# Two-layer hybrid backbone: where the second layer's modulation is multiplied

## The chip, the cores and the metric

One core of a Trainium2 chip runs the whole program. The metric is the time of one execution on the device, in microseconds (us); the time of a kernel is the median of its runs. TensorE is called PE, VectorE DVE, ScalarE ACT, GpSimd POOL, SyncE SP; PEld is PE's loading of weights.

## The reference

Two layers work on 256 context and 256 latent tokens of width 1024. Each layer has two sub-layers, a token mixer and a mixture of experts, and both read a modulated norm:

```python
mod_x = jnp.split((sc @ ada_w[l] + ada_b[l])[:, None, :], ADA_CHUNKS, axis=-1)
...
hx = modulate(xx, norm1_g[l], mod_x[0], mod_x[1])
mc, mx = token_mixer(hc, hx, p, lower[l], row, col, lam_init, last)
xx = xx + mod_x[2] * mx
hx = modulate(xx, norm2_g[l], mod_x[3], mod_x[4])
xx = xx + mod_x[5] * expert_choice_moe(hx, moe_router[l], moe_w1[l], moe_w3[l], moe_w2[l])
```

`sc` is silu of the condition (one vector for the latents, one for the context), `ada_w[l]` is 1024 x 6144: six chunks of 1024 columns, numbered 0 to 5. Chunks 0 and 1 are needed before the mixer, 2 at its end, 3 and 4 before the experts, 5 after them. The mixer has four branches, which all read the same modulated tokens through one wide projection: a gated linear attention (GLA) scan, a Hyena convolution, an HGRN2 scan, and a differential attention (two softmaxes, the second subtracted). Each branch's output is multiplied by its matrix, gated by a sigmoid of its own 1024 projected columns, and the four are summed (the merges) and projected out. The experts are 16, each of which takes its best tokens.

## The kernel before, in words

All weights are streamed in f32. Matmuls of the mixer are done as three products of split halves: a weight tile of 128x1024 (512 KB, SP's queue, `load`, L797 to L807) is split into a high part on ACT (L804) and a low part on DVE (L805), and then a column block is 24 matmuls of 128x128 by 128x256 (`col_block`, PSUM tag "d", two buffers). PSUM tags have fixed numbers of buffers: `BUFS = {"d": 2, "s": 3, "m": 2, "a": 1}`. In the trace a tile in PSUM is named by its tag: pd, ps, pm, pa.

A modulation chunk is eight tiles of 128x1024 of ada_w (512 KB each). `Ada.step` (L463 to L474) loads one tile by SP (L466) and multiplies it by the 32 condition columns, four matmuls side by side into 32 partitions each of one "a" tile; the trace records 8 matmuls for a tile. After eight tiles `mod_write` (L444 to L453) copies the result (DVE, L446), transposes it on PE (L425) and adds the bias (DVE, L453). In the second layer chunks 2 to 5 (32 tiles) are done by `AdaBack` (L477 to L495): it has two buffers of 1024 columns, and every call `run(n)` at some place of the mixer lets it do n tiles more. The constants at L31 to L35 set the places: two tiles in the turn and half a tile for each of the eight modulated blocks (`TR`), two with each mixer weight (`ADA`, L806), half with each step of the scans (`SCN`). In the trace all 32 tiles are done before the attention starts, so later calls do nothing.

The turn is the stretch from the last scatter of layer 0's experts to the first column blocks of layer 1 (gk, gq): sums of squares, norms (`rs_tokens`, `bcast_rs`, L760 to L763), modulation of the eight blocks (L764 ff.). Then come the weights in the order gk, gq, gv0, gv1, hq0 and so on: the GLA scan, the HGRN scan, the projections of the attention, the rotations, the attention.

The attention (L1187 to L1223) has eight iterations: four heads by two blocks of 128 queries. An iteration makes two scores on PE (tag "s", L1207), a maximum of each (DVE, L1209), its negative (L1210), an exponential of each with its sum (ACT, L1211), the reciprocals and the weighting (DVE, L1214 to L1216), transposes of the result (PE, tag "m", L1218), their copy (ACT, L1220), and the product with the values, accumulated over four iterations in one more "s" tile. After four iterations the output is normalised (L1230 to L1235, a chain of some twenty small DVE and ACT operations) and transposed (L1246, L1247).

The merges (`merge`, L853 to L872) of branches 0 and 2 follow in the source (L1266, L1267), those of 3 and 1 behind the Hyena branch. A merge has eight steps: column block, tanh (ACT, L858), product of six matmuls with the branch's matrix, and a gated sum (DVE, L866, L870). Which instruction comes when on an engine is decided by a scheduler over the whole program, which interleaves merge blocks with the attention; tiles and buffers are handed out in the order of the source. The product's PSUM tag is chosen at L863: "s" while modulation is left to do, else "a"; since none is left by then, it is "a".

## Time and profile before

| | us |
|---|---|
| median of 3 runs | 2025.32 |
| the runs | 2013.99, 2025.32, 2026.59 |
| the profiled execution | 2021.9 |
| its span in the trace | 2020.1 |
| PE busy in the span | 1859.6 (92%) |
| DVE busy | 801.5 (40%) |
| ACT busy | 526.1 (26%) |

How to read it: a table of stretches gives, for each stretch of the span, the time that each engine was busy (PE, PEld, DVE, ACT, POOL in this order) and in brackets the number of its instructions, then the granted clock of PE (1.00 is full), the share of the DMA engines and GB/s. A timeline row gives start, duration, engine, line, operation, the written tile and what it was read from, and in square brackets how long the engine stood idle before and what ended that. Line L428 is the helper that records every matmul, so matmuls are told apart by their tiles.

### The profile page before, as it was taken

Reading aid. Unit: us, or ns where it says so; the run is one execution under the profiler, and the core shown is the slowest. Engines: PE = TensorE matmul, PEld = TensorE weight load, DVE = VectorE, ACT = ScalarE, POOL = GpSimd, SP = SyncE. Lnnn points to the kernel's source line nnn. Section 1 sums busy time; section 2 is a strip of 40 time slices with the busy share of each in tenths; the row PEclk is TensorE's granted clock in tenths of the full one; section 3 lists DMA queues with packets and bytes.
Section 4 is the critical chain, followed back from the end, with each engine's and each line's share of the span. In section 5 each row is a group of like instructions: output and inputs, shape, how many; then the busy total and the mean of one; then the engine's idle time right before and its main releaser. Section 6 shows DMA issues by size and latency. Waiting matters only on the chain.

```text
span 2020.1 us, 28474 instructions
## 1 busy us (share of the span) xinstructions
PE 1859.6 (92%) x11722; PEld 1089.5 (54%) x11722; DVE 801.5 (40%) x1768; ACT 526.1 (26%) x929; POOL 28.7 (1%) x52
## 2 busy tenths in 40 slices
PE   7999999999999899999897889999998999987877
PEld 3666677887887434434232356788997333221213
DVE  5464638837543313212020345769865111110101
ACT  4432336622232211101000243447443100000000
POOL 0000000000000000000000010001000000000000
PEclk9998999999999899999999999999998999999999
DMA  8744531322326999999999856334568999999999
GB/s 310 224 151 135 177 102 58 105 84 84 122 98 260 359 401 350 380 409 409 409 409 409 314 188 199 105 102 139 198 251 326 409 409 409 409 409 409 409 409 332
DMA packets 154005, 549.03 MB, mean 272 GB/s; under 512 B 11026, under 2 KB 22674, under 8 KB 153108
## 3 DMA queue, kind: packets, MB, share of 16 engines
q1 hardware_dynamic: 153300, 544.08, 71.2%
q0 software_dynamic: 576, 3.15, 0.5%
q8 instruction: 92, 1.51, 0.3%
q14 instruction: 37, 0.30, 0.0%
HBM read 544.03 MB, written 3.15 MB: 271 GB/s over the span
## 4 chain that ended last, share of the span: by engine, by line
PE 71%; DMA 20%; DVE 5%; issue 2%; ACT 2%; SPq 0%; DVEq 0%; ACTq 0%
PE pd L428 41%; PE ps L428 15%; DMA r<-moe_w 9%; DMA base<-moe_w 7%; PE pm L428 6%; PE pa L428 6%; DMA base<-ada_w 2%; PE pm L425 2%; DMA base<-wg 1%; ACT r L804 1%; PE ps L1597 1%; DVE r L805 1%; DMA base<-xT 0%; DVE r L1195 0%; DVE base L1594 0%
## 5 line engine op out<-in xcount | busy, mean ns | idle before, releaser
L428 PE MATMUL pd<-r 128*128 128x256 f32 (+3 forms) x2976 | 572.3, 363 | 12.0 <-DMA r<-moe_w 7.6
L428 PEld LDWEIGHTS pd<-r 128*128 128x128 f32 (+2 forms) x2976 | 424.7, 184 | 132.0 <-issue 59.3
L428 PE MATMUL pd<-r,r 128*128 128x512 f32 (+3 forms) x1304 | 284.1, 435 | 12.0 <-DMA r<-moe_w 9.4
L805 DVE TENSOR_TENSOR r<-base,r 128x1024 fp32r<-128x1024 f32 x136 | 166.0, 1222 | 160.5 <-ACT r L804 157.4
L428 PEld LDWEIGHTS pd<-r,r 128*128 128x128 f32 (+2 forms) x1304 | 162.7, 167 | 107.6 <-issue 59.3
L804 ACT ACTIVATE r<-base 128x1024 fp32r<-128x1024 f32 x136 | 143.5, 1059 | 268.9 <-PE pd L428 216.2
L428 PE MATMUL ps<-base 32*64 32x64 f32 (+12 forms) x2372 | 178.3, 280 | 12.3 <-DMA base<-hy 4.4
L428 PE MATMUL pd<-r,base 128*32 128x512 f32 (+1 forms) x680 | 166.7, 598 | 12.0 <-DMA r<-moe_w 10.4
L428 PEld LDWEIGHTS ps<-base 32*64 32x64 f32 (+7 forms) x2372 | 113.2, 144 | 73.3 <-issue 43.3
L428 PE MATMUL pm<-base 128*128 128x128 f32 (+12 forms) x660 | 104.7, 326 | 18.3 <-DVE base L1528 5.8
L428 PE MATMUL ps<-r,base 128*64 128x512 f32 (+4 forms) x468 | 98.6, 525 | 13.7 <-DVE base L1598 6.3
L428 PE MATMUL pd<-base 128*32 128x512 f32 (+1 forms) x408 | 100.5, 595 | 6.4 <-DMA base<-moe_w 5.6
L428 PEld LDWEIGHTS pm<-base 128*128 128x128 f32 (+5 forms) x660 | 72.2, 179 | 61.2 <-issue 31.5
L428 PEld LDWEIGHTS pd<-r,base 128*32 128x32 f32 (+1 forms) x680 | 42.0, 122 | 112.1 <-issue 73.9
L1594 DVE TENSOR_TENSOR r<-base,pd 64x512 f32<-64x512 f32 x16 | 10.9, 680 | 214.4 <-PE pd L428 202.2
L1593 ACT ACTIVATE base<-pd 128x512 f32<-128x512 f32 (+1 forms) x32 | 19.0, 594 | 253.7 <-PE pd L428 253.7
L1594 DVE TENSOR_TENSOR base<-base,pd 128x512 f32<-128x512 f32 x16 | 11.0, 688 | 184.6 <-PE pd L428 150.4
L428 PE MATMUL pa<-r,r 128*128 128x512 f32 (+1 forms) x384 | 82.6, 342 | 1.1 <-DVE base L866 1.1
L1644 ACT ACTIVATE base<-ps 32x512 f32<-32x512 f32 (+2 forms) x28 | 14.7, 526 | 252.5 <-PE ps L428 248.0
L1644 ACT ACTIVATE r<-ps 32x512 f32<-32x512 f32 (+2 forms) x32 | 15.4, 480 | 249.9 <-PE ps L428 243.8
L428 PE MATMUL pd<-base,r 128*32 128x512 f32 (+1 forms) x296 | 71.3, 597 | 9.4 <-DMA base<-moe_w 9.4
L428 PE MATMUL pa<-base 128*32 128x256 f32 (+1 forms) x704 | 70.1, 407 | 9.4 <-DMA base<-ada_w 9.2
(241 smaller groups left out, 1633.6 us busy)
## 6 DMA issues: line engine op xcount, KB each, us to landing
r<-moe_w SPq DMA_DIRECT2D x251, 1024.0 KB, 18.2
base<-moe_w SPq DMA_DIRECT2D x131, 1024.0 KB, 17.9
base<-wg SPq DMA_DIRECT2D x152, 512.0 KB, 3.3
base<-ada_w SPq DMA_DIRECT2D x84, 512.0 KB, 4.6
r<-ada_w SPq DMA_DIRECT2D x12, 512.0 KB, 10.3
base<-xT SPq DMA_DIRECT2D x4, 1024.0 KB, 6.2
filters<-r SPq DMA_DIRECT2D x8, 256.0 KB, 4.3
base<-filters POOLq DMA_DIRECT2D x2, 1024.0 KB, 6.4
```

What stands on the lines that cost most here:

```text
L425: T.transpose(out, in_, ident)
L428: return T.matmul(out, lhsT, rhs, start=start, stop=stop, **kw)
L804: A.activation(w[0](), raw(), AF.Copy)
L805: V.tensor_tensor(w[1](), raw(), F(w[0]()), op=OP.subtract)
L1593: A.activation(s_(np_=rows), pa[0:rows, :], AF.Silu)
L1594: V.tensor_tensor(h_(np_=rows), s_(np_=rows), pb[0:rows, :], op=OP.mult)
L1597: T.transpose(p[:, q * rows:q * rows + rows], h_(q * 128, n=128, np_=rows), cs("ident", n=rows, np_=rows))
L1644: A.activation(dst, src, AF.Copy)
```

## The change

`AdaBack` is no longer used; the new `AdaBurst` takes its place. At the end of layer 0's experts it takes as many buffers of 1024 columns as memory gives, up to 16 (there are six), and loads the first tiles. In the turn, `turn` multiplies chunks 2 and 3 in one go (sixteen tiles) and frees the buffers. `run`, still called in `load` and the scans, does nothing. Ahead of the first merge it takes buffers again (there are fourteen) and loads eight tiles; `block`, called before each column block of the merges of branches 0 and 2, multiplies a whole chunk if eight tiles are under way or landed, and issues two more loads. Chunks 4 and 5 are done there. The products of these two merges take the PSUM tag "s".

```diff
--- before.py
+++ after.py
@@ -494,6 +494,63 @@
                 if not self.left:
                     self.buf.free()
 
+    class AdaBurst:
+
+
+        def __init__(self, chunks, per):
+            self.tiles, self.per = [(l, c, k) for l, c in chunks for k in range(KB)], per
+            self.left, self.issued, self.done, self.bufs = len(self.tiles), 0, 0, []
+
+        def run(self, n=None):
+            pass
+
+        def open(self, bufs):
+            self.bufs = bufs
+            self.load(KB)
+
+        def load(self, n):
+            while n and self.issued < len(self.tiles) and self.issued - self.done < len(self.bufs):
+                l, c, k = self.tiles[self.issued]
+                b = self.bufs[self.issued % len(self.bufs)]
+                S.dma_start(out=b(), in_=ins["ada_w"][l][128 * k:128 * k + 128, c * 1024:(c + 1) * 1024])
+                self.issued += 1
+                n -= 1
+
+        def chunk(self, more=0):
+
+            p = ps("a")
+            for k in range(KB):
+                l, c, _ = self.tiles[self.done]
+                b = self.bufs[self.done % len(self.bufs)]
+                for j in range(4):
+                    mm(p[32 * j:32 * j + 32, 0:256], cs_b(k * 32, n=32), b(j * 256, n=256), k == 0, k == KB - 1)
+                self.done += 1
+                self.left -= 1
+                if self.issued < more:
+                    self.load(1)
+            mod_write(l, c, p)
+
+        def block(self):
+
+            if self.issued - self.done >= KB:
+                self.chunk()
+            self.load(self.per)
+
+        def turn(self):
+
+            for _ in range(2):
+                self.chunk(2 * KB)
+            for b in self.bufs:
+                b.free()
+            self.bufs = []
+
+        def close(self):
+            while self.left:
+                self.block()
+            for b in self.bufs:
+                b.free()
+            self.bufs = []
+
 
     def rsqrt_small(x, n, y, t):
 
@@ -760,11 +817,9 @@
             b = rs_tokens(sums.tokens(mem), 2, mem)
             rs = bcast_rs(b, 2)
             b.free()
-            ada_bg.run(TR[1])
+            ada_bg.turn()
         for k in range(KB):
             t = tmp[k % 2]
-            if l:
-                ada_bg.run(TR[2])
             for s in range(2):
                 c = slice(s * 256, s * 256 + 256)
                 sc_, sh = Ac(k * 2 + s, n=1), mod[l](k * 2 + s, n=1)
@@ -850,15 +905,17 @@
             b = ob[br]
             split(src, b(2 * fb * W, n=W), b((2 * fb + 1) * W, n=W))
 
-        def merge(br, first):
+        def merge(br, first, burst=None):
             o = ob[br]
             for d in range(KB):
+                if burst:
+                    burst.block()
                 p = col_block(f"m{br}{d}", t0)
                 g = view(accb, d * W, W) if first and l else mem.take(W, keep_x if first else None)
                 A.activation(g(), p, AF.Tanh, scale=0.5)
                 if d % 4 == 0:
                     load_wb(br, d // 4)
-                p = ps("s" if ada_bg.left else "a")
+                p = ps("s" if ada_bg.left or burst else "a")
                 for fb in range(2):
                     w = [b(((d % 4) * 2 + fb) * 128, n=128) for b in wbs]
                     mm3(p[:, 0:W], w, (o(2 * fb * W, n=W), o((2 * fb + 1) * W, n=W)),
@@ -1261,11 +1318,25 @@
                 ahead.append(b)
 
         run_ahead(AHEAD[l][0])
-        if FL[l]:
+        burst = None
+        if l == 0:
             ada_bg.run()
-        merge(0, True)
-        merge(2, False)
-        ada_bg.run()
+        else:
+            burst = ada_bg
+            tmp, bufs = [mem.take(W) for _ in range(2)], []
+            while len(bufs) < 2 * KB:
+                try:
+                    bufs.append(mem.take(1024))
+                except MemoryError:
+                    break
+            for b in tmp:
+                b.free()
+            burst.open(bufs)
+        merge(0, True, burst)
+        merge(2, False, burst)
+        if burst:
+            burst.close()
 
 
         df, H = mem.take(1024), mem.take(2048)
@@ -1656,14 +1727,11 @@
                                            op0=OP.mult, op1=OP.add)
                 if not last and gr == 3:
                     if d == 0:
-                        b, keep = [b for b in slots if b.mem is mem][:2]
+                        b = [b for b in slots if b.mem is mem][0]
                         slots.remove(b)
                         spare.append(b)
-                        slots.remove(keep)
                         nxt.append(TokenSums(0, [view(b, 512 * i, 512) for i in range(4)], tag="s"))
-                        nxt.append(AdaBack([(1, c) for c in range(2, 6)], keep))
                     nxt[0].step(d)
-                    nxt[1].run(TR[0])
                 if last and gr == 3:
                     S.dma_start(out=outT[:, d * 256:d * 256 + 256], in_=xk(d, 1))
 
@@ -1690,7 +1758,20 @@
                     gather(gr + 1)
             if gr < 3:
                 scatter(gr)
-        for b in spare + slots + mid + [xg[1]] + gone + Pg + ys:
+        for b in slots + gone:
+            b.free()
+        mem.merge()
+        if not last:
+            nxt.append(AdaBurst([(1, c) for c in range(2, 6)], 2))
+            bufs = []
+            while len(bufs) < 2 * KB:
+                try:
+                    bufs.append(mem.take(1024))
+                except MemoryError:
+                    break
+            nxt[1].open(bufs)
+        for b in spare + mid + [xg[1]] + Pg + ys:
             b.free()
         mem.merge()
         dump(f"xmoe{l}", xb[0]())
```

How the change moves instructions is shown at three places. First PE from the end of the gk block on, in the kernel before (pd_6955 is gk, pd_6995 gq, pd_7062 and pd_7112 are the blocks behind, gv0 and gv1; pa_6985 is the second chunk, eight tiles):

```order
L428 MATMUL pd_6955<-r_6809 128x512 x4
L428 MATMUL pa_6985<-base 32x256 x8
L428 MATMUL pd_6995<-r_6809 128x256 x24
L428 MATMUL pm_7022<-base 128x512
L428 MATMUL pm_7026<-base 128x512
L428 MATMUL pa_6985<-base 32x256 x8
L428 MATMUL pd_7062<-r_6809 128x256 x38
L428 MATMUL pa_6985<-base 32x256 x4
L428 MATMUL pd_7062<-r_6809 128x256 x9
L428 MATMUL pa_6985<-base 32x256 x4
L428 MATMUL pd_7062<-r_6809 128x256
L428 MATMUL pd_7112<-r_6809 128x256 x48
```

There each four or eight matmuls of the chunk stand between column blocks. In the changed kernel the end of the turn reads (pd_7002 gk, pd_7031 gq, pd_7078 and pd_7128 the blocks behind, pa_6890 the second chunk):

```order
L428 MATMUL pd_7002<-r_6815 128x512 x3
L428 MATMUL pd_7031<-r_6815 128x256 x2
L428 MATMUL pa_6890<-base 32x256 x4
L428 MATMUL pd_7031<-r_6815 128x256 x9
L428 MATMUL pa_6890<-base 32x256 x4
L428 MATMUL pd_7031<-r_6815 128x256 x5
L425 MATMUL pm_6926<-base 128x128 x2
L428 MATMUL pd_7031<-r_6815 128x256 x8
L428 MATMUL pm_7058<-base 128x512
L428 MATMUL pm_7062<-base 128x512
L428 MATMUL ps_7183<-base 64x64 x3
L428 MATMUL pd_7078<-r_6815 128x256
L428 MATMUL pd_7128<-r_6815 128x256
```

What moved: the last six of sixteen tiles stand among gk and gq, and behind gq there is no pa tile until the merges.

Second, PE in the attention of the kernel before, around the second pair of scores (ps_8760 to ps_8818 are scores, ps_8724 the accumulated output, pd_9233, pd_9270 and pd_9307 column blocks of merges, pa_9222 and pa_9259 products of a merge):

```order
L428 MATMUL pa_9222<-r_7165,r_6813 128x256 x6
L428 MATMUL ps_8724<-base 128x64 x4
L428 MATMUL ps_8760<-r_7165 128x512
L428 MATMUL ps_8765<-r_7165 128x512
L428 MATMUL pd_9233<-r_6809 128x256 x22
L428 MATMUL pa_9259<-r_7165,r_6813 128x256 x6
L428 MATMUL ps_8795<-r_7165 128x512
L428 MATMUL pd_9270<-r_6809,r_6813 128x256 x2
L428 MATMUL ps_8800<-r_7165 128x512
L428 MATMUL pd_9307<-r_6809 128x256 x4
L428 MATMUL pd_9270<-r_6809,r_6813 128x256 x14
L428 MATMUL ps_8818<-r_7165 128x512
```

The blocks with their products stand between the iterations. In the changed kernel the same stretch reads (ps_8706 to ps_8784 are scores, ps_8630 the accumulated output, pm_ the transposed weights, pa_8916 chunk 4):

```order
L428 MATMUL ps_8706<-r_7181 128x512
L428 MATMUL pa_8916<-base 32x256 x3
L425 MATMUL pm_8679<-base 128x128 x4
L428 MATMUL ps_8724<-r_7181 128x512
L428 MATMUL ps_8729<-r_7181 128x512
L428 MATMUL ps_8630<-base 128x64 x4
L428 MATMUL ps_8779<-r_7181 128x512
L425 MATMUL pm_8714<-base 128x128 x4
L428 MATMUL ps_8784<-r_7181 128x512
L428 MATMUL ps_8630<-base 128x64 x4
L425 MATMUL pm_8737<-base 128x128 x4
L428 MATMUL ps_8630<-base 128x64 x4
```

What moved: no column block stands between the iterations from the second to the eighth, only tiles of chunk 4. Seven blocks stand ahead of the first transposes, the first product of a merge (ps_8989) stands behind the scores of the eighth iteration, and nine blocks stand behind the attention.

Third, SP's queue at the start of the second mixer before (L466 is a tile of ada_w, L803 a mixer weight):

```order
L466 DMA base<-ada_w 128x1024 x2
L803 DMA base<-wg 128x1024
L466 DMA base<-ada_w 128x1024 x2
L803 DMA base<-wg 128x1024
L466 DMA base<-ada_w 128x1024 x4
L803 DMA base<-wg 128x1024
L466 DMA base<-ada_w 128x1024 x2
```

and in the changed kernel, up to the first merge's weights (L515 is a tile of ada_w, L858 a mixer weight, L867 a branch's matrix):

```order
L515 DMA base<-ada_w 128x1024 x16
L858 DMA base<-wg 128x1024 x19
L867 DMA base<-wg 128x1024
L858 DMA base<-wg 128x1024 x6
L867 DMA base<-wg 128x1024
L858 DMA base<-wg 128x1024 x2
L515 DMA base<-ada_w 128x1024 x3
L858 DMA base<-wg 128x1024
L515 DMA base<-ada_w 128x1024 x3
L867 DMA base<-wg 128x1024
```

What moved: sixteen tiles are issued in one piece ahead of the mixer weights from gv0 on; the other sixteen stand among the weights of the first merges, behind which later weights queue.

## Rows read from the trace of the kernel before

**Rows 1.** Table of stretches: start:end, length, busy us (instructions) per engine.

```profile
1157.20:1190.50 33.30, 29.56 (x180) 13.26 (x180) 19.26 (x51) 10.64 (x22) 6.44 (x6) 0.90 0.64 209
1190.50:1209.10 18.60, 16.22 (x134) 12.82 (x132) 4.95 (x6) 10.53 (x13) 0.00 (x0) 1.00 0.56 193
1209.10:1235.00 25.90, 25.18 (x382) 14.91 (x382) 19.56 (x56) 10.38 (x24) 1.46 (x5) 1.00 0.61 201
...
1265.70:1283.20 17.50, 17.35 (x244) 13.03 (x243) 14.92 (x42) 9.24 (x20) 0.89 (x3) 1.00 0.36 122
```

**Rows 2.** The same stretches, PE's instructions on the pa tiles alone.

```profile
1157.20:1190.50 33.30, 8.45 (x80) 0.90 0.64 209
1190.50:1209.10 18.60, 2.56 (x32) 1.00 0.56 193
1209.10:1235.00 25.90, 7.55 (x72) 1.00 0.61 201
...
1246.00:1265.70 19.70, 2.35 (x32) 1.00 0.48 160
1265.70:1283.20 17.50, 2.56 (x32) 1.00 0.36 122
```

**Rows 3.** Timeline of PE in the turn, two tiles in a run.

```profile
1186.49 1.07 PE L428 MATMUL pa<-base 128*32 128x256 f32 x16
```

**Rows 4.** Waits of PE from 1190 to 1300 us: total, times, longest.

```profile
PE pa L428 <- DMA base<-ada_w: 3.8, 4, 2.2
```

**Rows 5.** DMA issues of the span: count, size, median us to landing.

```profile
base<-wg SPq DMA_DIRECT2D x152, 512.0 KB, 3.3
base<-ada_w SPq DMA_DIRECT2D x84, 512.0 KB, 4.6
```

**Rows 6.** Timeline of PE in the turn: the transposes of the norms.

```profile
1164.10 1.11 PE L425 MATMUL pm<-base 128*128 128x128 f32 x4 [2.23 <-DVE base L504]
```

**Rows 7.** Timeline of PE, end of the second merge: two blocks.

```profile
1431.68 3.04 PE L428 MATMUL pd<-r,r 128*128 128x256 f32 x24
1434.56 3.02 PE L428 MATMUL pd<-r 128*128 128x256 f32 x24
```

**Rows 8.** Table of stretches: attention and merges, columns as in rows 1.

```profile
1366.60:1434.60 68.00, 65.03 (x513) 62.24 (x514) 59.85 (x152) 44.53 (x85) 5.00 (x9) 1.00 0.45 156
```

**Rows 9.** Timeline of PE in the attention: scores, transposes, scores, scores, output.

```profile
1366.63 0.47 PE L428 MATMUL ps<-r 96*128 96x512 f32 x1 [0.18 <-DVE r L1195]
...
1378.96 0.63 PE L425 MATMUL pm<-base 128*128 128x128 f32 x4 [0.32 <-DVE base L1216]
...
1403.82 0.71 PE L428 MATMUL ps<-r 96*128 96x512 f32 x2
...
1409.85 0.40 PE L428 MATMUL ps<-r 96*128 96x512 f32 x1
...
1418.59 1.10 PE L428 MATMUL ps<-base 128*128 128x64 f32 x8
```

**Rows 10.** Timeline of DVE in the attention: maximum, its negative, weighting.

```profile
1407.68 0.67 DVE L1209 TENSOR_REDUCE base<-ps 128x1 f32<-128x512 f32 x1
...
1408.40 0.14 DVE L1210 TENSOR_SCALAR base<-base 128x1 f32<-128x1 f32 x1
...
1409.06 0.74 DVE L1216 SCALAR_TENSOR_TENSOR base<-base 128x512 f32<-128x512 f32 x1
```

**Rows 11.** Timeline of ACT in the attention: copy of the transposes, exponential.

```profile
1402.27 0.58 ACT L1220 ACTIVATE base<-pm 128x512 f32<-128x512 f32 x1
...
1405.86 0.69 ACT L1211 ACTIVATE base<-ps,base 128x512 f32<-128x512 f32 x1 [1.79 <-DVE base L1210]
```

**Rows 12.** Timelines of DVE and PE: last normalisation's start, transposes behind it.

```profile
1419.74 0.42 DVE L1230 TENSOR_TENSOR base<-ps,base 128x256 f32<-128x256 f32 x1 [1.15 <-PE ps L428]
...
1426.80 0.41 PE L425 MATMUL pm<-base 128*128 128x128 f32 x2
```

**Rows 13.** Table of stretches between mixer and experts, columns as in rows 1.

```profile
1540.00:1560.00 20.00, 11.27 (x93) 9.39 (x91) 11.56 (x44) 4.98 (x10) 0.00 (x0) 0.87 0.77 298
```

More of the change, by code (lines that the diff above doesn't have):

```diff
@@ L1263, in mixer @@
         run_ahead(AHEAD[l][0])
-        if FL[l]:
+        burst = None
+        if l == 0:
             ada_bg.run()
-        merge(0, True)
-        merge(2, False)
-        ada_bg.run()
+        else:
[8 more added lines that the diff above has]
+                b.free()
+            print("merge1", len(bufs))
+            burst.open(bufs)
[3 more added lines that the diff above has]
+            burst.close()
         df, H = mem.take(1024), mem.take(2048)
@@ L1692, in moe @@
                 scatter(gr)
-        for b in spare + slots + mid + [xg[1]] + gone + Pg + ys:
+        for b in slots + gone:
[9 more added lines that the diff above has]
+                    break
+            print("turn", len(bufs))
+            nxt[1].open(bufs)
+        for b in spare + mid + [xg[1]] + Pg + ys:
             b.free()
```

## The prediction

> **What bounds the kernel now.** I read the table of stretches first. TensorE (PE) is busy in nearly all of every stretch of the second mixer: 25.18 of 25.9 us in the GLA scan, 17.35 of 17.5 in the HGRN scan [rows 1]. So work put on PE there, or a wait put in front of it, moves the end. The experts of layer 1 begin where the mixer ends, so I let a microsecond gained or lost in the mixer count fully at the end (rival 3 is the case in which it doesn't).
>
> The same table for the modulation's tiles alone (PSUM name pa) shows where they stand: 80 of 256 records, that is 10 of 32 tiles at 8 records each, up to the end of the gq block, then 4 tiles, 9 in the GLA scan, 4 in the blocks between the scans, 4 in the HGRN scan [rows 2], and one between. A tile costs from 0.64 us (2.56 us for 4) to 0.84 us (7.55 us for 9) where it stands alone among small matmuls. In a run of 16 records it is 0.53 us [rows 3].
>
> The waits of PE from 1190 to 1300 us come last: 3.8 us for landing tiles, four times [rows 4]. A tile takes 4.6 us from issue to landing, a mixer weight 3.3 us [rows 5]. AdaBack has two buffers of 1024 columns, so only two are ever under way.
>
> **The change, part one: what leaves the scans.** All 32 tiles stay; 22 of them leave the stretch from 1190.5 to 1283.2 us.
> - The waits for landing tiles: 3.8 us gained [rows 4].
> - Eight or nine tiles beside column blocks, where PE has no other limit: 2.56 us in 1190.5 to 1209.1, 2.35 us in 1246 to 1265.7 [rows 2], and one tile between, 0.8 us. Together 5.7 us busy, of which I take 5.0; at the packed price (0.53 us) it is 4.8.
> - Nine tiles in the GLA scan: 7.55 us of PE. But VectorE (DVE) is busy 19.56 of the 25.9 us [rows 1] in the scan's own chain, so the most to be had is 25.9 - 19.6 = 6.3 us and the least nothing; I take 3.5, about the middle, since PE and DVE of a scan wait for each other in turn.
> - Four tiles in the HGRN scan: DVE 14.92 of 17.5, so 0 to 2.6 us; I take 1.2.
>
> In the scans, then, the row gives 3.5 and 1.2 us for taking PE work away, because PE is the fuller engine there (25.18 against 19.56 us). The Trainium skill, page "Perfetto Trace Analysis", section "Optimization Strategy", speaks against that: where a kernel has regimes with different limits, it says, interleaving them can pay. By it the tiles lie rightly beside the scans' vector work, nothing is gained there, and the sum below would be 4.7 us higher; the rows agree only in part, since PE is as full as it can be.
>
> **Part two: the turn.** Sixteen tiles now stand among the sums of squares, the gk and the gq block, ten before. Six more at 0.84 us are 5.1 us. PE has a gap of 2.23 us there before the transposes of the norms [rows 6], and PE is busy 29.56 of 33.3 us [rows 1], so a part of the six is free; between 0 and -5.1 I take -2.5. The six buffers are loaded from the end of the experts on. SyncE's queue issues all sixteen loads in one piece ahead of the weights of gv0; the sixteenth needs the buffer of the tenth tile, which PE's order has in the middle of gk and gq, so gv0's weights are not later than now. If they were, the price is one landing, 3.3 us [rows 5].
>
> Gain so far: 3.8 + 5.0 + 3.5 + 1.2 - 2.5 = 11.0 us; with the ends of each term 3.5 to 18.4 us.
>
> **Part three: the merges and the attention.** This decides. In the kernel before, sixteen merge blocks (24 matmuls each, 2.88 us start to start [rows 7]) and their products stand on PE between the eight iterations of the attention. From the first score to the end of the second merge it is 68.0 us with PE busy 65.03 [rows 8]: the chain of an iteration is hidden. In the changed one three things happen.
> - Sixteen tiles come in, most in runs of 8 to 24 matmuls: 16 x 0.53 = 8.5 us of PE (13.4 at 0.84).
> - The products now take the PSUM tag "s" (three buffers) in place of "a". The attention's scores and its accumulated output take "s" too, so the first product stands behind the scores of the eighth iteration. Tanh, product and sum of a block can't finish, but the blocks themselves run ahead: seven of them are done before the first transposes of the attention.
> - The eighth block's weights queue on SyncE behind tiles that wait for memory that the attention still holds. So from the second iteration to the eighth PE has no block at all to do.
>
> PE's own work in those seven iterations is: scores 0.71, transposes 0.63, output 1.10 [rows 9], 2.44 us each, 17.1 in all; with five tiles (2.7) and four products of six matmuls (0.72 each, a quarter of a block's 2.88: 2.9) 22.7 us. The chain of an iteration, all in line, is 0.71 + 0.67 + 0.67 (two maxima) + 0.14 + 0.69 + 0.69 (two exponentials) + 0.74 + 0.63 + 0.58 (copy) + 1.10 = 6.6 us [rows 9 to 11]. Where the kernel now is fastest, three score pairs come 6.03 us apart from first to third, 3.0 us an iteration [rows 9]. With one of three "s" buffers held by the output, one pair is in flight: scores, maxima, one small operation and both exponentials, 3.6 us, before the next. To that I add 0.8 us for the tiles and products that stand between (5.6 us over seven): 4.4 us, nearer to the 3.0 than to the 6.6. Seven times 4.4 is 31 us, so 8 us of PE lie idle (at 3.0 none, at 6.6, 46 us, 23).
>
> Before the first transposes the chain from the second score (about 5 us: maxima, exponentials, weighting) has two blocks as cover, but DVE is then still at the second half's rotations; in the present trace it took from 1366.63 to 1378.96 [rows 9]. I take 3 us idle (0 to 6). After the last output comes the normalisation: from 1419.74 to the transposes at 1426.80 it is 7.1 us [rows 12], now hidden by two blocks. Then the tiles and weights that waited for the attention's memory have to land (4.6 and 3.3 us [rows 5]). Seven products and some tiles cover a part; I take 4 us idle (0 to 10).
>
> Sum of the stage: 8.5 + 8 + 3 + 4 - 3.0 (the idle time that it has now, 68.0 - 65.03) = +20.5 us. The Hyena stage behind it has fewer blocks left beside its convolutions; I put 2 us on it (0 to 5).
>
> **The sum.** 20.5 + 2 - 11 = +11.5 us. The profiled execution took 2021.9 us (its span is 2020.1): 2033.4. The median of the three runs is 3.4 us above it and they spread over 12.6 us, so I say 2037.
>
> **Rivals.**
> 1. *The attention hides itself (not slower).* If iterations come every 3.0 us, as in [rows 9], PE's 22.7 us of work is the longer and the 8 us idle are gone; with the scans shortened to DVE's time the gain is 16, near its upper end of 18.4. For it: the pace of 3.0 us was reached with DVE and ACT serving blocks as well, which they no longer do. Against it: at that pace two pairs overlapped only because other PE work let the chain run ahead, and the order has none. Time: 8.5 + 7 - 3 + 0 - 16 = -3.5, so 2018 on the profiled run, 2015 to 2022. It decides from a pace under 3.2 us.
> 2. *The attention is serial (clearly slower).* At 6 us an iteration seven take 42 us, 11 us more than I count. With PE busy 22.7 of 42 us the clock may fall as well: the stretch 1540 to 1560, busy 11.27 of 20, shows a mean granted clock of 0.87, part of it then at 1.2 in place of 2.4 GHz [rows 13], where 16.22 of 18.6 us busy still show 1.00 [rows 1]. At 0.87 22.7 us of matmul cost 3.4 more. 2037 + 11 + 3 = 2051. The Trainium skill, page "TensorE: Matmul & The Clock Gate", section "Why this matters for your kernels", warns of idle gaps between bursts of matmuls; the two rows agree. For it: the three "s" buffers. Against: DVE and ACT are nearly free of block work in that time.
> 3. *It changes nothing that counts.* Tiles are moved, PE's sum is the same, and the blocks that no longer cover the attention cover the tiles. The gain of 11 then stands against 8.5 + 2, or a shift of the mixer is taken up by the experts' weight stream: 2025. Against it: the order has no block between the iterations.
>
> **How the numbers follow.** Forecast 0.50, rival 1 0.14, rival 2 0.24, rival 3 0.12. A measurement of this kernel can tell about 1%, 20 us, from no change. Forecast and rival 3 stay within it, save the upper fifth of the forecast (losses over 2045); rival 2 lies mostly above; rival 1 rarely goes 20 us below. So slower by over 1%: 0.8 x 0.24 + 0.2 x 0.50 = 0.29; faster 0.07; within 0.64. The range goes from 2014 (rival 1) to 2056 (rival 2 with the tiles at 0.84 us); the forecast's own is 2026 to 2048.
>
> **What would show it.** In the changed profile: no pa tile from the end of gq to the merges, the GLA scan near 22 us, no wait for ada_w there; the time from first score to last output with PE idle a third of it and waits for DVE and ACT (maxima, exponentials, copies); the blocks of the second merge after it back to back; the stage from the first score to the end of the second merge near 89 us in place of 68. If that stage is under 75 us, part three is wrong; if the scans are as long as now, part one is.

## The result, and the profile after

| | before | changed |
|---|---|---|
| median, us (5 runs each) | 2025.32 | 2054.59 |
| runs, us | 2013.99 to 2028.48 | 2044.12 to 2057.08 |
| ratio, 95% interval | | 1.0146 (1.0105 to 1.0187) |
| profiled execution, us | 2021.9 | 2044.12 |

The changed kernel is slower by 1.5%, 29 us by the medians. Its profiled execution is the fastest of its five, so the two traces lie only 22 us apart.

The table of stretches of the changed kernel (columns as in [rows 1]: length, then busy us with counts of PE, PEld, DVE, ACT, POOL, then granted clock, DMA share, GB/s). The first three stretches run from the sums of squares in the turn to the first score of the attention, from there to the end of the attention's last output, and from there to the end of the second merge; the fourth is a part of the second. The end of the second merge is taken one column block behind its last product, in every trace alike.

```profile
1155.10:1348.80 193.70, 184.54 (x1670) 140.22 (x1670) 123.61 (x307) 87.67 (x172) 17.19 (x27) 0.99 0.33 111
1348.80:1402.60 53.80, 42.60 (x237) 32.11 (x238) 34.37 (x102) 26.29 (x58) 3.17 (x6) 0.75 0.40 125
1402.60:1453.90 51.30, 46.89 (x405) 41.82 (x404) 29.18 (x57) 17.73 (x25) 1.16 (x2) 0.97 0.63 204
1372.80:1396.80 24.00, 19.23 (x76) 13.66 (x76) 13.81 (x45) 10.15 (x25) 0.00 (x0) 0.55 0.09 25
```

The same three stretches of the kernel before, from the same view:

```profile
1160.80:1366.60 205.80, 194.58 (x1798) 141.92 (x1798) 123.83 (x314) 86.49 (x170) 15.56 (x26) 0.98 0.45 150
1366.60:1419.70 53.10, 50.12 (x389) 47.51 (x390) 48.69 (x124) 38.41 (x75) 5.00 (x9) 1.00 0.40 139
1419.70:1434.60 14.90, 14.90 (x125) 14.73 (x125) 11.16 (x28) 6.12 (x10) 0.00 (x0) 1.00 0.62 213
```

Up to the first score the change gains 12.1 us (205.8 to 193.7). The attention (first score to last output) lasts as long as before, 53.8 against 53.1 us, but in it PE carries out 237 matmuls in place of 389, and for 24 us of it its mean granted clock is 0.55. What isn't done there comes behind: 51.3 against 14.9 us. Together the two stretches, which answer to [rows 8], take 37 us more. The rest differs by little: the changed trace enters the turn 5.7 us earlier, a stretch that the change doesn't touch, and needs 2.6 us more from the end of the second merge to the end. Without the 5.7 us the traces differ by 28 us, near the 29 of the medians.

The modulation's tiles alone in the changed kernel, columns as in [rows 2]: none between gq and the attention, 128 records (sixteen tiles) in the attention and behind it.

```profile
1187.20:1345.10 157.90, 0.00 (x0) 0.99 0.26 90
1348.80:1402.60 53.80, 5.74 (x48) 0.75 0.40 125
1402.60:1453.90 51.30, 6.09 (x80) 0.97 0.63 204
```

The longest waits of PE in the changed kernel from the first score to the end of the second merge (total, times, longest; L1268 is the exponential, L1277 the copy of the transposes):

```profile
PE pa L428 <- DMA base<-ada_w: 3.4, 4, 1.8
PE ps L428 <- ACT base L1268: 2.8, 4, 2.1
PE ps L428 <- ACT base L1277: 2.4, 4, 0.7
PE pd L428 <- DVE r L860: 2.1, 1, 2.1
```

The waits for landing tiles have moved, not gone: 3.8 us in the scans before [rows 4], 3.4 us here. The timeline of PE inside the attention of the changed kernel, transposes (pm), outputs (x8) and scores (96x512):

```profile
1375.43 1.97 PE L428 MATMUL ps<-base 128*128 128x64 f32 x8
1377.19 1.06 PE L425 MATMUL pm<-base 128*128 128x128 f32 x4
1379.00 1.97 PE L428 MATMUL ps<-base 128*128 128x64 f32 x8 [0.75 <-ACT base L1277]
1380.76 1.06 PE L425 MATMUL pm<-base 128*128 128x128 f32 x4
1382.57 1.97 PE L428 MATMUL ps<-base 128*128 128x64 f32 x8 [0.75 <-ACT base L1277]
1384.30 1.20 PE L428 MATMUL ps<-r 96*128 96x512 f32 x2
1387.56 0.76 PE L428 MATMUL ps<-r 96*128 96x512 f32 x1 [2.06 <-ACT base L1268]
```

An output takes 1.97 us where it took 1.10 [rows 9], four transposes 1.06 where they took 0.63. No column block stands between; PE goes from one small step to the next and waits for the copy or the exponentials.

The pace of the attention is read from the starts of its eight outputs. The first, second, fifth and sixth of the kernel before (the eighth, at 1418.59, is in [rows 9]):

```profile
1380.33 1.10 PE L428 MATMUL ps<-base 128*128 128x64 f32 x8
1389.95 1.10 PE L428 MATMUL ps<-base 128*128 128x64 f32 x8
1402.90 1.10 PE L428 MATMUL ps<-base 128*128 128x64 f32 x8
1411.78 1.10 PE L428 MATMUL ps<-base 128*128 128x64 f32 x8
```

and the first, second, sixth and eighth of the changed kernel (the fifth, at 1382.57, is above):

```profile
1363.16 1.10 PE L428 MATMUL ps<-base 128*128 128x64 f32 x8 [0.73 <-ACT base L1277]
1372.24 1.10 PE L428 MATMUL ps<-base 128*128 128x64 f32 x8 [0.20 <-ACT base L1277]
1393.60 1.97 PE L428 MATMUL ps<-base 128*128 128x64 f32 x8
1401.52 1.10 PE L428 MATMUL ps<-base 128*128 128x64 f32 x8
```

From first to last it is 38.3 us before and 38.4 in the changed kernel. In both, two steps are long, the first to the second output (9.6 and 9.1 us) and the fifth to the sixth (8.9 and 11.0).

### The profile page after: what moved, and what is told of

It reads as the page before. It is cut to its first block, busy times and chain, and to the rows that moved or that the text cites. A ratio compares the mean times of both kernels' runs of the same rounds, so it can differ in the third digit from the quotient of the medians.

```text
span 2042.0 us, 28467 instructions
## 1 busy us (share of the span) xinstructions
PE 1868.6 (92%) x11722; PEld 1096.2 (54%) x11722; DVE 805.2 (39%) x1768; ACT 526.7 (26%) x929; POOL 29.7 (1%) x52
## 4 chain that ended last, share of the span: by engine, by line
PE 71%; DMA 19%; DVE 5%; issue 2%; ACT 2%; SPq 0%; DVEq 0%; ACTq 0%
PE pd L428 41%; PE ps L428 15%; DMA r<-moe_w 9%; DMA base<-moe_w 7%; PE pm L428 6%; PE pa L428 5%; DMA base<-ada_w 2%; PE pm L425 2%; DMA base<-wg 1%; DVE r L860 1%; ACT r L859 1%; PE ps L1668 1%; DMA base<-xT 0%; DVE r L1252 0%; ACT r L1250 0%
## 5 line engine op out<-in xcount | busy, mean ns | idle before, releaser
L428 PE MATMUL pd<-r,r 128*128 128x512 f32 (+3 forms) x1304 | 281.6, 433 | 11.8 <-DMA r<-moe_w 9.4
L1715 ACT ACTIVATE r<-ps 32x512 f32<-32x512 f32 (+2 forms) x32 | 15.4, 480 | 250.1 <-PE ps L428 243.9
L428 PEld LDWEIGHTS ps<-r,base 128*64 128x64 f32 (+2 forms) x468 | 32.8, 140 | 68.9 <-issue 43.5
```

The costliest lines, as they stand in the source:

```text
L428: return T.matmul(out, lhsT, rhs, start=start, stop=stop, **kw)
L1715: A.activation(dst, src, AF.Copy)
```

## The experiments

All are compared with the kernel before on the same chip. Of a kernel's edit the lines that matter are shown; "..." stands for lines left out. "Stage" is the time from the first score to the end of the second merge (67.9 us before, 105.1 us in the changed kernel). Theory T says that the merge products, and with them the blocks, wait for a PSUM buffer that the attention holds; rival R that the sixteen tiles and their loads among the merges cost the time.

| kernel | median, us | ratio to before (95%) |
|---|---|---|
| s_only | 2051.41 | 1.0130 (1.0110 to 1.0150) |
| prod_a | 2064.42 | 1.0176 (1.0148 to 1.0203) |
| prod_a_m | 2028.19 | 1.0019 (1.0001 to 1.0038) |
| turn_only | 2037.54 | 1.0052 (1.0025 to 1.0079) |
| burst_only | 2058.03 | 1.0155 (1.0124 to 1.0187) |
| s_warm | 2065.87 | 1.0189 (1.0160 to 1.0218) |
| late | 2029.54 | 1.0009 (0.9993 to 1.0026) |
| turn_back2 | 2035.65 | 1.0043 (1.0025 to 1.0062) |
| s_nr4 | 2069.86 | 1.0228 (1.0196 to 1.0261) |
| turn6 | 2032.67 | 1.0027 (1.0007 to 1.0046) |
| back6 | 2017.26 | 0.9959 (0.9938 to 0.9979) |
| back4 | 2018.04 | 0.9957 (0.9937 to 0.9977) |

### Which buffer the products take

**s_only**: one condition in the kernel before.

```diff
-                p = ps("s" if ada_bg.left else "a")
+                p = ps("s" if ada_bg.left or (l and br in (0, 2)) else "a")
```

Expected: 

> The kernel before with one word changed: the products of the merges of branches 0 and 2 in layer 1 take PSUM tag s in place of a; the modulation stays in the scans. Theory T (the products wait for the attention's own s tiles, so blocks, tanh and sums back up and nothing covers the attention): 22 to 30 us slower than before, some 2050, first score to end of the second merge near 96 us, and a low granted clock in the attention. Rival R (the sixteen tiles and their loads in the merges cost the time): no change, 2025.

Measured: 2051, and a stage of 97.8 us. Its two stretches, first score to last output and from there to the end of the second merge:

```profile
1365.50:1420.00 54.50, 39.71 (x180) 32.87 (x180) 33.38 (x101) 25.97 (x58) 3.71 (x7) 0.62 0.13 44
1420.00:1463.30 43.30, 40.67 (x327) 39.39 (x328) 28.78 (x52) 18.52 (x26) 0.00 (x0) 1.00 0.53 168
```

No tile of ada_w has moved, yet the picture is that of the changed kernel: 180 matmuls in the attention, a clock of 0.62, the blocks behind it. So the tag alone, without a single tile in the merges, costs 30 us of the 37, and by difference the sixteen tiles and their loads the other 7.

**prod_a**: the changed kernel with the products on "a".

```diff
-                p = ps("s" if ada_bg.left or burst else "a")
+                p = ps("a")
...
```

Expected: 

> The changed kernel with the merge products back on tag a, which the two chunks use too. If tag s alone is the holder: about 2028, since the attention gets its blocks back. Theory T in its wider form (whatever buffer the product needs must not be held by something that ends with the attention; a is held by chunk 4, whose last tiles wait for memory that the attention holds): as the changed kernel, 2050 to 2057. Rival R: 2054.

Measured: 2064, slower even than the wider form of T had it, and no sign of the 2028. The two stretches:

```profile
1354.80:1408.00 53.20, 39.98 (x210) 27.50 (x210) 32.76 (x98) 26.04 (x58) 3.19 (x6) 0.73 0.39 123
1408.00:1474.30 66.30, 57.45 (x430) 50.19 (x431) 31.25 (x61) 17.98 (x26) 1.15 (x2) 0.81 0.51 160
```

Tag "s" isn't special. "a" has one buffer and the program hands it to chunk 4 first; chunk 4 ends only when its last tiles have found memory that the attention gives back (two of their loads stand 12.9 and 16.7 us on SyncE's queue until operations of the attention are done), and every product stands behind it: the first starts at 1417.1, behind the last output at 1408.0.

**prod_a_m**: the chunks of the merges on "m" as well, the products on "a".

```diff
-            p = ps("a")
+            p = ps("m" if not more else "a")
...
-                p = ps("s" if ada_bg.left or burst else "a")
+                p = ps("a")
...
```

Expected: 

> The changed kernel with the merge products on tag a and the two chunks in the merges on tag m, where only short transposes stand. The same tiles, loads and turn. Theory T: the blocks stand between the attention's iterations again, 12 us gained before the first score stay, 8.5 us of tiles come back: 2020 to 2028. Rival R: still over 2045.

Measured: 2028, with the same tiles, loads and turn as the changed kernel. The two stretches (of an execution of 2020, the fastest of its ten):

```profile
1349.40:1399.80 50.40, 46.23 (x351) 42.88 (x351) 45.04 (x119) 35.08 (x71) 4.36 (x8) 1.00 0.54 180
1399.80:1430.60 30.80, 28.37 (x296) 23.63 (x295) 16.79 (x41) 9.27 (x14) 1.16 (x2) 1.00 0.81 282
```

The blocks are back between the iterations, the clock is 1.00, and the stage takes 81.2 us. Against 67.9 the sixteen tiles cost 13 us here: PE is busy 9.6 us more (46.23 + 28.37 against 65.03), and the rest is idle time (50.40 - 46.23 and 30.80 - 28.37, together 6.6, against 3.0 before). 12 us gained and 13 lost leave nothing. The theory of the buffer holds.

### Which part of the change

How far one trace can be trusted here: s_only and s_warm (below) have the same program up to the first score, and from the turn to there their traces take 207.5 and 211.6 us. The changed kernel, prod_a, prod_a_m and late agree better: 193.7, 194.8, 193.8 and 192.6. A difference of 4 us in this stretch, read from one trace each, shows nothing. The stretch in s_only, s_warm and four kernels of this section (turn_only, turn_back2, turn6, burst_only, in this order):

```profile
1158.00:1365.50 207.50, 194.67 (x1804) 142.25 (x1804) 124.80 (x314) 87.88 (x172) 17.49 (x28) 0.99 0.46 151
1158.40:1370.00 211.60, 197.26 (x1803) 143.43 (x1804) 124.94 (x314) 88.03 (x172) 16.86 (x28) 0.98 0.46 148
1163.70:1377.90 214.20, 200.59 (x1797) 145.07 (x1797) 125.13 (x313) 86.70 (x170) 15.94 (x27) 0.96 0.43 136
1157.90:1374.50 216.60, 202.62 (x1796) 147.23 (x1796) 124.33 (x314) 86.78 (x170) 14.66 (x26) 0.94 0.42 135
1161.70:1374.30 212.60, 196.28 (x1797) 144.71 (x1797) 124.67 (x314) 86.49 (x170) 15.22 (x26) 0.97 0.41 135
1159.60:1357.10 197.50, 184.62 (x1674) 139.14 (x1675) 123.33 (x307) 87.82 (x172) 16.84 (x27) 0.98 0.37 121
```

**turn_only**: chunks 2 and 3 in the turn as in the change, chunks 4 and 5 through two of the six buffers as before.

```diff
...
-            for b in self.bufs:
+            for b in self.bufs[2:]:
                 b.free()
-            self.bufs = []
+            return AdaTail([(1, 4), (1, 5)], self.bufs[:2])
...
```

`AdaTail` is `AdaBack` with a list of buffers of its own.

Expected: 

> Part of the change alone: chunks 2 and 3 in one go in the turn, chunks 4 and 5 as before, two tiles with each mixer weight through two buffers, done long before the merges; products on tag a. Where the scans pay for emptied PE (12.2 us for 22 tiles in the changed kernel): 6 tiles leave them and the waits halve, 3 to 7 us faster than before, 2018 to 2022. If the gain there was the burst's loads alone: no change, 2025.

Measured: 2038, a miss on both sides. From the turn to the first score it takes 214.2 us, where before takes 205.8. For as many records PE is busy 6.0 us longer (200.59 against 194.58), at a granted clock of 0.96 in place of 0.98, and idle 2.4 us longer. SyncE's queue behind the turn in turn_only (start, duration; L466 a tile, L868 a mixer weight):

```profile
1196.68 2.67 SPq L466 DMA_DIRECT2D base<-ada_w  x2
1199.44 0.38 SPq L868 DMA_DIRECT2D base<-wg  x1
1201.33 4.67 SPq L466 DMA_DIRECT2D base<-ada_w  x2
1206.05 0.42 SPq L868 DMA_DIRECT2D base<-wg  x1
```

The two buffers are busy with the last tiles of the turn, so the queue stands at a tile's load, 2.67 and 4.67 us, and the weights of the next blocks stand behind it. PE then waits 3.26 us for a tile (1204.53), and that tile takes 1.08 in place of 0.64 us.

**turn_back2** lets the tail start two mixer weights later (against turn_only).

```diff
...
-            self.chunks, self.raw, self.buf, self.credit, self.n = todo, bufs, self, 0, 0
+            self.chunks, self.raw, self.buf, self.credit, self.n = todo, bufs, self, -4, 0
...
```

Expected: 

> turn_only with the loads of chunk 4 not queued ahead of gv0's weights: AdaTail starts two mixer weights later. If the 5 us wait behind gq in turn_only (and the half clock after it) was the queue: the wait goes, 2025 to 2030. If tiles in the scans cost more where they stand in a piece of sixteen: as turn_only, 2037.

Measured: 2036 (216.7 us from the turn to the first score): the explanation by gv0's weights alone falls.

**turn6** keeps all six buffers for the tail (against turn_only).

```diff
...
-            for b in self.bufs[2:]:
-                b.free()
-            return AdaTail([(1, 4), (1, 5)], self.bufs[:2])
+            return AdaTail([(1, 4), (1, 5)], self.bufs)
...
```

Expected: 

> turn_only with all six buffers kept for chunks 4 and 5 in the scans in place of two. If turn_only was slow because two buffers let SyncE's queue stand at a tile's load with mixer weights behind it: as back6 or a little better, 2015 to 2022. If sixteen tiles in the turn are themselves too many: 2028 or more.

Measured: 2033 (212.6 us). A little better than turn_only, if at all (the intervals overlap), and far from back6 below. Four tiles' loads stand here ahead of gv0's weights, and soon behind gq PE is busy only 4.29 of ten us at a clock of 0.58:

```profile
1201.70:1211.70 10.00, 4.29 (x60) 2.95 (x64) 7.47 (x13) 5.43 (x9) 0.00 (x0) 0.58 0.96 386
```

Against back6 (197.2 us, 190.95 of them busy), which has the same tiles and as many buffers, turn6 loses 15.4 us: 10.1 of idle time and 5.3 of longer records. That sixteen tiles in one piece ahead of more tiles in the scans is a bad order, these three kernels show; which wait brings it about stays open.

**burst_only**: the other part alone, chunks 4 and 5 as in the change, 2 and 3 by `AdaBack`.

```diff
...
-            burst = ada_bg
+            ada_bg.run()
+            burst = AdaBurst([(1, 4), (1, 5)], 2)
...
```

Expected: 

> The other part of the change alone: chunks 2 and 3 through two buffers in the turn and behind it as before, chunks 4 and 5 in bursts among the merges of branches 0 and 2 with the products on tag s. Theory T: the attention's loss of 31 us and 7 us for the tiles stay, sixteen tiles less in the scans give back 8 to 12 us: 2050 to 2058. Rival (the loss comes from the turn's burst): 2025 or less.

Measured: 2058, at the upper end; the turn to the first score takes 197.5 us, so sixteen tiles fewer there, still with two buffers, give 8.3 of the 12.1 us. The other 3.8 would be the burst's in the turn, but single traces differ by as much.

**late**: the turn as in the change, products on "a", chunks 4 and 5 on "m" among the merges of branches 3 and 1.

```diff
...
+            burst.open(bufs)
         run_ahead(AHEAD[l][1])
...
-        merge(3, False)
-        merge(1, False)
+        merge(3, False, burst)
+        merge(1, False, burst)
...
```

Expected: 

> The turn as in the changed kernel; chunks 4 and 5 on tag m among the merges of branches 3 and 1, after the attention and the Hyena branch, where column blocks stand back to back; all merge products on tag a. Theory T: the attention is as in the kernel before, 12 us gained before the first score stay, sixteen tiles cost 8.5 us of PE: 2019 to 2024. Rival (tiles cost as much as in prod_a_m, 15 us, wherever they stand in the merges): 2027 to 2030.

Measured: 2030, the rival's number. From the turn to the first score 192.6 us, so the gain is there; but from there to the last merge product 166.4 against 153.1 us, 13 again. PE is busy 9.7 us more there, 0.60 us a tile, and idle 3.6 us more, of which one wait of 2.26 us for the first tile is the largest part. With the idle time around it a tile costs some 0.8 us here, as in prod_a_m, against the 0.53 of a packed run.

### What the slow clock costs

**s_warm**: s_only with filler on PE ahead of each iteration, to keep the clock up.

```diff
...
+                    if l and ei[1]:
+                        p, ep = ps("a"), es[(ei[1] - 1) % 3]
+                        for i in range(FILL):
+                            j = i % 4
+                            mm(p[32 * j:32 * j + 32, 0:256], cs_b(0, n=32), ep[1](0, n=256), True, True)
...
```

Expected: 

> The kernel s_only (merge products on tag s) with filler: ahead of each attention iteration from the second on 16 small matmuls (32 recorded, some 2.1 us at full clock) that read the iteration before and write a PSUM tile that nothing reads; so 15 us of PE work more than s_only, which shows a granted clock of 0.50 for some 30 us. Theory C (the half clock is a part of the loss, and PE's idle is what brings it): clock over 0.9 in the attention, first to last output 30 to 36 us in place of 39.1, total 3 to 9 us faster than s_only, some 2045. Rival (the chain on DVE and ACT sets the pace, the clock only stretches PE's idle): first to last output 39 us or more, total as s_only or up to 10 us slower.

Measured: 2066, 48.1 us from the first to the last output where s_only takes 39.1. Theory C's numbers fail: the clock rose in a part only (between 0.65 and 1.00 in stretches of 12 us). Two iterations of s_warm in which it did (lines are one further than in s_only; the pa row is the filler):

```profile
1406.15 1.10 PE L429 MATMUL ps<-base 128*128 128x64 f32 x8 [0.75 <-ACT base L1226]
1407.18 1.93 PE L429 MATMUL pa<-base 128*32 128x256 f32 x32
1409.05 0.66 PE L426 MATMUL pm<-base 128*128 128x128 f32 x4
1410.45 1.10 PE L429 MATMUL ps<-base 128*128 128x64 f32 x8 [0.75 <-ACT base L1226]
```

From output to output 4.30 us, of which the filler (1407.18 to 1409.05) takes 1.87, so 2.43 without it. The like step of the changed kernel at the slow clock takes 3.57 (1375.43 to 1379.00 above). By that the slow clock would cost about 1.1 us an iteration, an estimate of at most 8 us for seven. But the filler stands on PE between an output and the next transposes, on the chain that it was to help, so the run doesn't settle it.

### What stops the blocks at the seventh

**s_nr4**: s_only with four raw weight buffers.

```diff
-    NR = 3
+    NR = 4
...
```

Expected: 

> The kernel s_only with a fourth buffer for the raw mixer weights. Theory: the blocks stop at the seventh because the eighth one's weights take the raw buffer that still holds the second half of the branch's matrix, and this is split only when the products before it are done. With four buffers one block more fits in between: 2.9 us less behind the last output, 2046 to 2050. Rival (the blocks are stopped by something else): as s_only, 2051.

Measured: 2070 in all, a miss: the turn begins 16 us later (1174.1 against 1158.0), so layer 0 lost them, where the fourth buffer leaves less memory; how was not looked into. Behind the turn the theory holds: the products stand behind the attention as in s_only, but one block more is done before (24 matmuls more on the pd tiles up to the last output), and from the last output to the last merge product it takes 126.8 us in place of 129.4, 2.6 less. In s_only SyncE's queue shows the same directly, in its longest wait from 1365 to 1430 us:

```profile
SPq L803 <- DVE base L1232: 47.8, 1, 47.8
```

That load, of a mixer weight, is issued at 1424.0, where the split of the matrix's second half ends on DVE (L680; the view names the operation next to it).

### A version that beats both

**back6** leaves each tile where the source had it before and replaces the two buffers by six, which are taken at the end of layer 0's experts, where memory is freed as in the changed kernel, and kept until the last tile.

```diff
...
-                self.cur.step(self.raw[self.n % 2])
+                self.cur.step(self.raw[self.n % len(self.raw)])
...
+            nxt.append(AdaTail([(1, c) for c in range(2, 6)], [mem.take(1024) for _ in range(6)]))
...
```

Expected: 

> The kernel before with nothing moved to another place of the source, but with six buffers of 1024 columns for the modulation's tiles in place of two, kept through the scans. If the waits for landing tiles are what the burst saves in the scans: the 3.8 us of waits go, 2021 to 2023. If the gain of the changed kernel there was only that tiles leave the scans: no change, 2025 to 2027.

Measured: 2017, 0.4% faster than before and more than the waits alone. **back4** is the same with four.

Expected: 

> back6 with four buffers. If four tiles under way cover a landing (4.6 us at about one tile each 1.3 us of transfer): as back6, 2015 to 2020. If the gain grows with each buffer: 2020 to 2023.

Measured: 2018. Its stretches from the turn to the first score and over the attention, and the one wait left for tiles from 1190 to 1300 us:

```profile
1160.70:1359.00 198.30, 191.41 (x1796) 142.08 (x1796) 124.24 (x314) 85.77 (x170) 14.48 (x25) 1.00 0.45 150
1359.00:1412.20 53.20, 50.12 (x380) 47.68 (x380) 48.79 (x124) 37.79 (x75) 5.62 (x10) 0.97 0.38 124
```

```profile
PE pa L428 <- DMA base<-ada_w: 0.9, 2, 0.5
```

With all 32 tiles in the turn and the scans it reaches the first score in 198.3 us, 7.5 less than before; 0.9 us of waits are left of 3.8, and the granted clock of the stretch is 1.00 in place of 0.98. Of the 7.5 us, 4.3 are idle time and 3.2 shorter records (191.41 against 194.58 us busy). Four buffers are enough: 2018 with four and 2017 with six, at a landing of 4.6 us [rows 5].

## Why the prediction was right in part

The forecast was 2037 and the range 2014 to 2056; 2054.6 came out. The side was right and so was the mechanism, a cover taken from the attention, but the likeliest case was too mild: the stage was put at +20.5 us and came out at +37.2. What came is nearest to rival 2 (0.24), and a loss of over 1% had been given 0.29 against 0.64 for a change within 1%. Two stretches of the changed kernel, first score to first transposes and first to last output:

```profile
1348.80:1361.80 13.00, 9.93 (x65) 8.78 (x66) 11.09 (x31) 7.92 (x15) 1.19 (x2) 0.87 0.73 219
1363.20:1401.50 38.30, 30.93 (x159) 21.82 (x159) 22.49 (x70) 17.06 (x41) 1.98 (x4) 0.69 0.26 87
```

- **The scans and the turn (11.0 us gained)**: 12.1 measured. The turn's part was put at -2.5; gq ends 32.1 us after the sums of squares in place of 29.7, so -2.4. No tile is left in the scans. The sum is right, its split isn't, and that is luck: back4, which leaves all 32 tiles in place and only has more buffers, gains 7.5 us by itself, so ending the waits is worth more than the 3.8 put down for them; with the waits gone, moving the tiles gives only another 4.6 (198.3 to 193.7; back6 has 197.2, prod_a, prod_a_m and late 192.6 to 194.8), where 7.2 (9.7 - 2.5) were counted.
- **The idle time of the stage (8 + 3 + 4 - 3 = 12 us)**: 15.6 against 3.0, so 12.6 measured. Right in its parts too: 3.1 us before the first transposes (13.00 - 9.93), 7.4 from the first to the last output (38.30 - 30.93), 4.4 behind the attention (51.30 - 46.89).
- **PE's own work (8.5 us more for the sixteen tiles, nothing more for the rest)**: this is the term that was mis-sized. PE is busy 89.5 us (42.60 + 46.89) in place of 65.0, 24.5 more. The tiles' records take 11.8 of it; the other 12.7 are longer records of the same work. Most of that is the clock: 19.23 us busy at 0.55 hold 10.6 us of work at full clock, an estimate of 8.7 us more. The forecast counted PE's work at full speed ("PE's own work in those seven iterations ... 22.7 us"), where 30.93 were measured at 0.69, and kept the clock for rival 2, at 3.4 us.
- **The pace (4.4 us an iteration, 31 us)**: 38.4 us from the first to the last output, 5.5 us an iteration, against 38.3 before with blocks between, 36.4 in prod_a_m and 39.1 in s_only. The forecast had the attention run faster once the blocks were gone. It doesn't. Its 3.0 us came from the fastest three score pairs; the trace of before, from its first to its last output, already had the 5.5, with the same two long steps. So the loss is the block work that no longer lies beneath it. Why the uncovered attention isn't faster, whether by the slow clock alone, was not settled.
- **The Hyena stage (2 us)**: 2.6 us, from the end of the second merge to the end of the kernel. With the terms above -12.1 + 37.2 + 2.6 = +27.7 us in place of +11.5.
- **"The eighth block's weights queue on SyncE behind tiles that wait for memory"**: not the wait that ends last. s_only has no such tiles and stops at the seventh block too. The raw buffer that the eighth weight needs still holds the second half of the branch's matrix, which is split only when the products of the first half are done (s_nr4). In the changed kernel the weight does stand behind tiles, but it is issued (1405.5) 2 us behind the last of them, when that split is done.
- **The tag**: "the first product stands behind the scores of the eighth iteration" was right, and s_only shows that it carries 30 of the 37 us.
- **The rivals**: rival 1 (pace of 3.0 us) fell. Rival 2 had 6 us an iteration and a clock of 0.87; 5.5 and 0.69 came. Rival 3 fell too: from the last merge product to the end it takes 500 to 504 us in every kernel run here, so a shift of the mixer comes through in full.
- **The rules of the Trainium skill**: the Trainium skill, page "Perfetto Trace Analysis", section "Optimization Strategy", was set against the gain in the scans. As it was put there, with nothing gained by clearing the scans, 6.3 us (11.0 - 4.7) would have come; 12.1 came, but back4 has 7.5 of them with every tile left in the scans, so the run doesn't refute the rule. As advice where to put the tiles it agrees: in the scans with four buffers they cost the first score 4.6 us more than the changed kernel (198.3 against 193.7), among the merges 13 (prod_a_m, late). The Trainium skill, page "TensorE: Matmul & The Clock Gate", section "Why this matters for your kernels", warns of idle gaps between bursts of matmuls. The clock did fall, to 0.55; but the longest gap in that stretch is 2.06 us (timeline above), and no run here shows that the gaps were the reason.

## What to carry to other kernels

In this program a named PSUM buffer is a queue in the order of the source: before moving a product to another tag, ask who holds that tag ahead of it and when he lets go, for everything behind the product backs up with it. Cover that lies between the steps of a chain can be worth its whole length: here the chain ran no faster without it (38.4 against 38.3 us). Where a stream makes an engine wait, try more buffers before another place for the work: here four buffers in place of two gave 0.4%, and moving the tiles gave nothing or a loss.

## What was not expected of the hardware

TensorE's mean granted clock was 0.55 over 24 us of the attention, the lower of its two levels (1.2 and 2.4 GHz) for nearly the whole stretch, while its records show it busy 19.23 of 24.00 us. Just before, in 12 us at 0.97, PE was busy 8.68 us; in the second half of the stretch the lower level held throughout:

```profile
1360.80:1372.80 12.00, 8.68 (x67) 5.13 (x66) 6.68 (x20) 6.66 (x16) 1.98 (x4) 0.97 0.54 199
1384.80:1396.80 12.00, 9.24 (x33) 5.41 (x32) 7.11 (x24) 5.05 (x13) 0.00 (x0) 0.50 0.06 17
```

At that level the records themselves are longer (1.97 for 1.10 us, 1.06 for 0.63), so a busy share of 80% hides a half-empty engine: the same work at full clock would be about 10.6 of 24 us, an estimate (19.23 x 0.55). The share of busy time and the clock have to be read together.
